# Hybrid decoder layer on one core: the sums of squares of the first half's tokens taken over features by TensorE in PSUM instead of by adds on VectorE and GpSimd

## The chip, the cores and the metric

The kernel runs on one core of one Trainium2 chip. Its engines are named as in the profile: PE (TensorE's matmuls) and PEld (its weight loads), DVE (VectorE), ACT (ScalarE), POOL (GpSimd) and SP (SyncE, which issues all of this kernel's DMAs). The metric is the time of one execution on the device in microseconds, the median of several runs, lower is better.

## The reference

One decoder layer over 2048 tokens of 1024 features, in float32. The step that matters here is the first line of the layer and what is multiplied by it:

```python
def rmsnorm(x, g):
    xf = x.astype(jnp.float32)
    y = xf * lax.rsqrt(jnp.mean(xf * xf, axis=-1, keepdims=True) + RMS_EPS)
    return (y * g.astype(jnp.float32)).astype(x.dtype)
...
h = rmsnorm(x, pre_g)
proj = h @ w_in
```

The columns of `proj` then feed three groups of heads: stick-breaking attention, sparse attention (an indexer scores all keys of a query, the best 256 are kept), and attention into 256 memory tokens. Their gated outputs go through one output projection, a second RMS norm and the residual. So for each token the sum of its 1024 squares must be formed, and its reciprocal root is a factor on everything the input projection yields.

## The kernel before

**Layout.** The input projection works on transposed tokens: `xT` has the features on the 128 partitions, in 8 tiles (`kt` = 0 to 7) of 128 features, and the tokens in 4 chunks `c` of 512. Each float32 operand is split into a high and a low part, and `three` multiplies hi by hi, hi by lo and lo by hi, so one output tile of 512 columns takes 8 x 3 = 24 matmuls into one PSUM bank. Banks are called `pp`, `pz`, `pT` and `po`, two of each; a unit whose tag has no free bank may borrow one of another tag.

**First half.** The program handles chunks 0 and 1 first (segment 0), then 2 and 3, then 0 and 1 again. `hprep_first` (L869) prepares a chunk of segment 0: for each `kt` it loads `xt`, makes `hi` (ACT or DVE) and `lo` (DVE) from x times the norm's weight, without the token's factor. Matmuls can thus start before any norm is known. Then it squares `xt` in place on ACT, adds the 8 squared tiles pairwise into two (`xs[0]`, `xs[1]`: even `kt` on DVE, odd on POOL), and lets PE sum these two over the partitions: for each of the 4 blocks `j` of 128 tokens, two matmuls with the block of squares as the weights and one column of ones as the moving operand. The four sums per partition go through `rstd` (DVE, then a power on POOL), `spread` transposes them on PE into a tile that ACT copies to SBUF (`rb`), and only then can an output tile of segment 0 leave its PSUM bank (`ev_split`, `nat_a`). Chunks 2 and 3 get their factors in another way (`factors`, L924: ACT squares `x` in token order, tiles named `Q`, and accumulates along the row).

**What runs around it.** `SEGMENTS` (L137) lists the units. In segment 0: `i0`, `i1` (the indexer's queries, four output tiles for the two chunks), then `q0` and `k0` together and `a0` (natural order, four token blocks, each 24 matmuls of 296 columns into one bank, then an eviction of eight steps by ACT and DVE), then `a1` and the rest.

**What sets the order.** The code yields operations; `Plan.run` (L518) is a list scheduler that prices each of them (L346; an fp32 matmul at 222 ns at the least) and emits, for each engine, one fixed order before anything runs. `either` offers an operation to two engines. Line L501 emits every operation, so nearly all rows of the profile name that line, and operations are told apart by their tiles. On the chip each engine goes through its list in order, and waits on semaphores.

**Names.** In the rows, `A`, `B` hold `xT` tiles and their squares, `H` the hi and lo parts, `R` the weights of `i0`, `i1`, `S` those of `q0`, `k0`, `V` and `W` those of `a0`, `Q` the raw loads (weights `wt`, or `x` for `factors`), `E` the tiles of evictions and of `rb`, `C` the small tiles of sums and factors. Tiles of the pool `xr` hold `xT`: 12 slots for the 16 tiles of chunks 0 and 1, so the last four loads of chunk 1 wait until tiles of chunk 0 are free.

Of the kernel before, what the change touches and what calls it, by code (L numbers as in the profile page):

```python
# [11 lines left out]
F32 = mybir.dt.float32  # L12
# [5 lines left out]
OP = mybir.AluOpType  # L18
# [4 lines left out]
P = 128  # L23
# [16 lines left out]
def rd(ap):  # L40
    return ap.bitcast(F32)
# [526 lines left out]
class Net:  # L568
# [48 lines left out]
    def consts(self):  # L617
        nc, a = self.nc, self.a
        pk = self.cload("pack", [P, 305], a["c_pack"])
        at = 0  # L620

        def part(w):
            nonlocal at
            at += w
            return pk[:, at - w:at]

        self.ident, self.causal, self.zt, self.stp = part(P), part(P), part(NB), part(NB)
        self.kvg, self.iota8, self.g = part(1), part(8), part(8)
        self.ones = self.cst.tile([P, P], F32, name="ones")
        nc.vector.memset(self.ones, 1.0)  # L630
        self.half = self.cst.tile([P, 16], F32, name="half")
        nc.vector.memset(self.half, 0.5)
        self.mhalf = self.cst.tile([P, 16], F32, name="mhalf")
        nc.vector.memset(self.mhalf, -0.5)
        self.fill = self.cst.tile([P, 1], F32, name="fill")
        nc.vector.memset(self.fill, FILL)
        self.mneg = self.cst.tile([P, 1], F32, name="mneg")
        nc.vector.memset(self.mneg, NEGM)
        self.zero = self.cst.tile([P, 1], F32, name="zero")
        nc.vector.memset(self.zero, 0.0)  # L640
        warm = self.cst.tile([P, 1], F32, name="warm")
        nc.scalar.activation(warm, self.zero, AF.Sigmoid)
        self.flags = self.cst.tile([P, NB], F32, name="flags")
        nc.vector.memset(self.flags, 0.0)
        self.far = self.cst.tile([P, NB, 6], F32, name="far")
        nc.gpsimd.memset(self.far, 0.0)
        c = lambda n, s, dt=F32: self.cst.tile(list(s), dt, name=n)
        self.identr = c("identr", [P, P], F32R)
        self.notyet = c("notyet", [P, P], F32R)
        self.iwt = [c(f"iw{k}", [P, 4, 8]) for k in range(NCH)]  # L650
# [218 lines left out]
    def hprep_first(self, c):  # L869

        pl = self.pl
        xs, H = [], []
        for kt in range(8):
            hi = yield Alloc("hh", [P, 512], F32R)
            lo = yield Alloc("hl", [P, 512], F32R)
            xt = yield Alloc("xr", [P, 512], F32)
            yield pl.sp.dma_start(xt, self.a["xT"][kt * P:(kt + 1) * P, c * 512:(c + 1) * 512])
            g = self.g[:, kt:kt + 1]
            yield pl.either(pl.act.activation(hi, xt, AF.Identity, scale=g, prio=2 * c),
                            pl.dve.tensor_scalar(hi, xt, g, None, op0=OP.mult, prio=2 * c))  # L880
            yield pl.dve.scalar_tensor_tensor(lo, xt, g, rd(hi), op0=OP.mult, op1=OP.subtract, prio=2 * c)
            xs.append(xt)
            H.append((hi, lo))
        pl.objs["H", 0, c] = H
        rb = yield Alloc("ev", [P, 512], F32)
        for kt in range(8):
            yield pl.act.activation(xs[kt], xs[kt], AF.Square, prio=2 * c + 1)
            if kt > 1:
                eng = pl.pool if kt % 2 else pl.dve
                yield eng.tensor_tensor(xs[kt % 2], xs[kt % 2], xs[kt], op=OP.add, prio=2 * c + 1)  # L890
                pl.F(xs[kt])
        if c == 1:
            self.stage("x")
        ps = yield Alloc("pT", [P, 512], F32)
        for j in range(4):
            for x in range(2):
                yield pl.pe.matmul(ps[:, j:j + 1], xs[x][:, j * P:(j + 1) * P], self.ones[:, 0:1], start=x == 0, stop=x == 1,
                                   prio=0)
        pl.F(*xs[:2])
        ss = yield Alloc("sm4", [P, 4], F32)  # L900
        yield pl.dve.tensor_copy(ss, ps[:, 0:4], prio=0)
        pl.F(ps)
        r = yield from self.rstd(ss, 4, 1.0 / D)
        pl.F(ss)
        yield from self.spread(r, rb)
        yield pl.sp.dma_start(self.RB[c], rb, wt=[("RB", c)])
        pl.objs["r", c] = (r, rb)
        if c == 1:
            self.stage("r")
# [1137 lines left out]
```

## Time and profile before

| | us |
|---|---|
| median of 3 runs | 1440.29 (1438.8 to 1441.74) |
| the profiled execution, its own time | 1438.55 |
| its span on the core | 1436.7 |
| PE busy | 1357.6 (94% of the span) |
| DVE busy | 1129.8 (79%) |
| ACT busy | 962.0 (67%) |
| POOL busy | 505.7 (35%) |

The profiled execution is 1.85 us longer than its span, and 1.74 us below the median of the runs. PE is the busiest engine, but its idle time is not spread evenly: of the first 80 us it is busy for 55.9 us, and from 200 to 300 us for 97.4 of 100. The change lies wholly in the first 60 us.

### The profile page before, as it was taken

How to read it: one execution, taken by the hardware profiler on the slowest of the kernel's cores; microseconds unless marked ns; L12 is line 12 of the kernel's file. 1: busy time of each engine (PE TensorE's matmuls, PEld its weight loads, DVE VectorE, ACT ScalarE, POOL GpSimd, SP SyncE). 2: the span in 40 equal slices, each digit the busy share in tenths (PEclk: the TensorE clock that was granted, in tenths of full speed). 3: DMA queues.
4: the chain of work that ended last, by engine and by line, in shares of the span. 5: the costliest groups of instructions: out<-in, count | busy, mean ns of one | idle time of the engine just before them, and what ended most of it. 6: DMA issues, size and time to landing. Idle time of an engine off the chain costs nothing.

```text
span 1436.7 us, 25178 instructions
## 1 busy us (share of the span) xinstructions
PE 1357.6 (94%) x7662; PEld 1151.3 (80%) x7662; DVE 1129.8 (79%) x3244; ACT 962.0 (67%) x2158; POOL 505.7 (35%) x693
## 2 busy tenths in 40 slices
PE   7688899999999899999999998889999999999996
PEld 5576678888888688978888886678888889898885
DVE  5437889889888899989887757889978898896332
ACT  6436677768778787888777749888766656765121
POOL 5516612223333337223445533444223221221452
PEclk9899999999999999999999999999999999999998
DMA  7638545766966347455768659886645483522563
GB/s 262 222 101 244 171 139 162 211 184 196 266 178 200 114 143 224 141 165 153 237 195 257 175 190 298 277 260 183 223 134 169 149 254 92 173 71 88 163 193 102
DMA packets 222781, 264.26 MB, mean 184 GB/s; under 512 B 17670, under 2 KB 141996, under 8 KB 222636
## 3 DMA queue, kind: packets, MB, share of 16 engines
q1 hardware_dynamic: 222636, 262.56, 60.1%
q8 instruction: 63, 1.03, 0.3%
q14 instruction: 82, 0.67, 0.1%
HBM read 183.58 MB, written 78.91 MB: 183 GB/s over the span
## 4 chain that ended last, share of the span: by engine, by line
PE 73%; ACT 7%; DVE 7%; DMA 4%; issue 2%; POOL 1%; SPq 0%; ACTq 0%; DVEq 0%; POOLq 0%
PE pp L501 43%; PE po L501 11%; PE pz L501 10%; PE pT L501 9%; DVE K L501 1%; DVE A L501 1%; ACT E L501 1%; ACT J L501 1%; DVE E L501 1%; DVE D L501 1%; POOL H L501 1%; ACT A L501 1%; DMA Q<-wt 1%; ACT V L501 1%; DVE C L501 1%
## 5 line engine op out<-in xcount | busy, mean ns | idle before, releaser
L501 PE MATMUL pp<-H,R 128*128 128x512 f32 x2328 | 636.5, 401 | 12.5 <-ACT H L501 8.1
L501 PEld LDWEIGHTS pp<-H,R 128*128 128x128 f32 x2328 | 425.4, 190 | 92.3 <-ACT H L501 9.2
L501 POOL TENSOR_TENSOR R<-Q,R 128x512 fp32r<-128x512 f32 x80 | 103.7, 1298 | 211.4 <-DVE R L501 68.6
L501 ACT ACTIVATE pz<-pz 128x512 f32<-128x512 f32 (+3 forms) x234 | 118.8, 514 | 29.1 <-PE pz L501 27.7
L501 POOL TENSOR_TENSOR V<-S,U 128x256 f32<-128x256 bf16 x48 | 32.6, 679 | 184.1 <-DVE C L501 166.6
L501 PE MATMUL pp<-W,H 128*128 128x296 f32 (+1 forms) x448 | 93.0, 293 | 0.0
L501 PE MATMUL po<-K,B 128*128 128x256 f32 (+3 forms) x352 | 85.6, 305 | 4.6 <-ACT K L501 1.7
L501 ACT CAST K<-pT 128x512 fp32r<-128x512 f32 (+3 forms) x135 | 61.3, 465 | 37.5 <-PE pT L501 28.9
L501 ACT ACTIVATE J<-A,D 128x384 uint8<-128x384 f32 (+9 forms) x60 | 75.3, 1255 | 15.8 <-DVE D L501 15.2
L501 ACT ACTIVATE E<-pp 128x512 f32<-128x512 f32 (+2 forms) x85 | 48.2, 567 | 48.9 <-PE pp L501 46.9
L501 PE MATMUL pp<-V,H 128*128 128x296 f32 (+1 forms) x320 | 71.1, 297 | 9.2 <-DVE E L501 9.2
L501 PE MATMUL pT<-pack,T 128*128 128x128 f32 x326 | 75.8, 275 | 0.4 <-DVE D L501 0.4
L501 PEld LDWEIGHTS po<-K,B 128*128 128x128 f32 x352 | 60.4, 192 | 15.4 <-ACT K L501 3.2
L501 DVE SCALAR_TENSOR_TENSOR A<-pz,iw,A 128x512 f32<-128x512 f32 (+3 forms) x105 | 70.1, 668 | 3.2 <-ACT pz L501 0.3
L501 PEld LDWEIGHTS pp<-W,H 128*128 128x128 f32 x448 | 71.3, 189 | 0.9
L501 POOL TENSOR_TENSOR T<-T 128x384 f32<-128x384 f32 (+2 forms) x42 | 34.5, 822 | 97.5 <-DVE T L501 77.5
L501 PEld LDWEIGHTS pp<-V,H 128*128 128x128 f32 x320 | 53.6, 189 | 13.2 <-DVE E L501 12.7
L501 PE MATMUL pz<-K,B 128*128 128x512 f32 (+3 forms) x158 | 60.0, 387 | 3.4 <-DMA B<-iq 1.3
L501 PE MATMUL pz<-H,R 128*128 128x512 f32 x192 | 61.5, 412 | 0.4 <-DVE C L501 0.4
L501 DVE TENSOR_SCALAR D<-D 128x1 uint8<-128x1 f32 (+1 forms) x308 | 42.3, 164 | 20.4 <-ACT J L501 17.1
L501 POOL TENSOR_TENSOR R<-E,R 128x512 fp32r<-128x512 f32 x25 | 33.5, 1342 | 68.9 <-ACT R L501 50.8
L501 ACT ACTIVATE pT<-pT 128x512 f32<-128x512 f32 (+3 forms) x99 | 51.6, 524 | 8.5 <-PE pT L501 7.7
(499 smaller groups left out, 3852.1 us busy)
## 6 DMA issues: line engine op xcount, KB each, us to landing
Q<-wt SPq DMA_DIRECT2D x84, 256.0 KB, 4.1
B<-qd SPq DMA_DIRECT2D x19, 512.0 KB, 5.8
S<-qsb SPq DMA_DIRECT2D x34, 256.0 KB, 4.3
B<-vd SPq DMA_DIRECT2D x33, 256.0 KB, 3.3
gt<-E SPq DMA_DIRECT2D x32, 256.0 KB, 3.1
S<-vsb SPq DMA_DIRECT2D x30, 256.0 KB, 4.3
S<-ksb SPq DMA_DIRECT2D x29, 256.0 KB, 4.7
B<-iq SPq DMA_DIRECT2D x56, 128.0 KB, 3.8
```

The costliest lines, as they stand in the source:

```text
L501: o.fn(*o.args, **o.kw)
```

## The change

For chunks 0 and 1 the twelve adds on DVE and POOL go. Instead PE sums all eight squared tiles of a chunk into the same four PSUM columns: a matmul of a tile of zeros opens the accumulation and another closes it, and between them stand 8 x 4 matmuls with a block of squares as weights and one column of ones as the moving operand. Each tile of squares is released when its four matmuls are done. The bank `pT` is taken before the squares instead of behind the adds. The whole diff:

```diff
@@ -638,6 +638,8 @@
         nc.vector.memset(self.mneg, NEGM)
         self.zero = self.cst.tile([P, 1], F32, name="zero")
         nc.vector.memset(self.zero, 0.0)
+        self.zero4 = self.cst.tile([P, 4], F32, name="zero4")
+        nc.vector.memset(self.zero4, 0.0)
         warm = self.cst.tile([P, 1], F32, name="warm")
@@ -883,20 +885,18 @@
             H.append((hi, lo))
         pl.objs["H", 0, c] = H
         rb = yield Alloc("ev", [P, 512], F32)
+        ps = yield Alloc("pT", [P, 512], F32)
         for kt in range(8):
             yield pl.act.activation(xs[kt], xs[kt], AF.Square, prio=2 * c + 1)
-            if kt > 1:
-                eng = pl.pool if kt % 2 else pl.dve
-                yield eng.tensor_tensor(xs[kt % 2], xs[kt % 2], xs[kt], op=OP.add, prio=2 * c + 1)
-                pl.F(xs[kt])
+            if kt == 0:
+                yield pl.pe.matmul(ps[:, 0:4], self.ones, self.zero4, start=True, stop=False, prio=0)
+            for j in range(4):
+                yield pl.pe.matmul(ps[:, j:j + 1], xs[kt][:, j * P:(j + 1) * P], self.ones[:, 0:1], start=False, stop=False,
+                                   skip_group_check=True, prio=0)
+            pl.F(xs[kt])
+        yield pl.pe.matmul(ps[:, 0:4], self.ones, self.zero4, start=False, stop=True, prio=0)
         if c == 1:
             self.stage("x")
-        ps = yield Alloc("pT", [P, 512], F32)
-        for j in range(4):
-            for x in range(2):
-                yield pl.pe.matmul(ps[:, j:j + 1], xs[x][:, j * P:(j + 1) * P], self.ones[:, 0:1], start=x == 0, stop=x == 1,
-                                   prio=0)
-        pl.F(*xs[:2])
         ss = yield Alloc("sm4", [P, 4], F32)
         yield pl.dve.tensor_copy(ss, ps[:, 0:4], prio=0)
```

The scheduler lays the whole program anew. On PE the first 197 instructions become 249; behind them PE's order is the same as before, and so are those of POOL and SP behind their first 38 and 61. Numbers behind a name only tell buffers apart; a row with x16 stands for sixteen instructions.

On PE, chunk 0: before, seven of the eight sums of chunk 0 (`pT0<-ones`) stand behind the matmuls of `i0` and `i1` on `kt` 0 to 3 of that chunk (`pp1` and `pp0`), and those of chunk 1 (`pz`) follow.

```order
L501 MATMUL pp0_110<-H3_125,R_120 128x512
L501 MATMUL pp0_110<-H2_124,R_120 128x512 x2
L501 MATMUL pp0_110<-H3_125,R_120 128x512
L501 MATMUL pT0_114<-ones_80,A1_123 128x1 x7
L501 MATMUL pz0_112<-H5_130,R_120 128x512
L501 MATMUL pz0_112<-H4_129,R_120 128x512 x2
```

On PE, chunk 0, now: the sums stand between the matmuls of `i0` (`pp1`), with only ten of its 24 ahead of the last of them.

```order
L501 MATMUL pp1_113<-H0_123,R_122 128x512
L501 MATMUL pT0_116<-ones_80,A1_125 128x1 x4
L501 MATMUL pp1_113<-H0_123,R_122 128x512
L501 MATMUL pT0_116<-ones_80,A1_125 128x1 x4
L501 MATMUL pp1_113<-H1_124,R_122 128x512
L501 MATMUL pp1_113<-H0_123,R_122 128x512 x2
L501 MATMUL pT0_116<-ones_80,A1_125 128x1 x8
L501 MATMUL pT0_116<-ones_80,A2_128 128x1 x16
L501 MATMUL pT0_116<-zero4_92,ones_80 128x4
L501 MATMUL pp1_113<-H1_124,R_122 128x512
```

The sums of chunk 0 moved from behind 38 matmuls of 512 columns to behind ten.

On PE, chunk 1: before, its sums (`B0`) stand behind all four tiles of `i0` and `i1`, and `q0` (weights `S`) follows.

```order
L501 MATMUL pz1_113<-H7_133,R_120 128x512
L501 MATMUL pz1_113<-H6_132,R_120 128x512
L501 MATMUL pT0_114<-ones_80,B0_131 128x1
L501 MATMUL pT1_115<-pack_78,C_128 128x128 x4
L501 MATMUL pT0_114<-ones_80,B0_131 128x1 x7
L501 MATMUL pp1_111<-H0_121,S_407 128x512
```

On PE, chunk 1, now: they stand in one piece ahead of the last matmul of `i1` on chunk 0 (`pp0`) and of all 24 of `i1` on chunk 1 (`pz1`).

```order
L501 MATMUL pp0_112<-H3_127,R_122 128x512
L501 MATMUL pT0_116<-ones_80,B0_132 128x1 x16
L501 MATMUL pT0_116<-ones_80,A1_125 128x1 x16
L501 MATMUL pT0_116<-zero4_92,ones_80 128x4
L501 MATMUL pp0_112<-H2_126,R_122 128x512
L501 MATMUL pz1_115<-H4_130,R_122 128x512
```

Twenty-five matmuls of 512 columns moved from ahead of these sums to behind them.

On DVE, the eviction of `a0`'s first block: before, the scaling of `pz1` and a cast of `S` stand ahead of its three steps (`iw0`, `B4`, and `E1` from `pp0`).

```order
L501 SCALAR_TENSOR_TENSOR E3_140<-pz0_112,E2_138 128x512
L501 SCALAR_TENSOR_TENSOR E1_137<-pz1_113,E2_138 128x512
L501 CAST S_407<-Q_119 128x512
L501 TENSOR_SCALAR iw0_100<-pp0_110,C_128 128x8
L501 SCALAR_TENSOR_TENSOR B4_485<-pp0_110,C_128,B4_485 128x2x32
L501 SCALAR_TENSOR_TENSOR E1_515<-pp0_110,C_128,E1_515 128x2x64
```

On DVE, the same place now.

```order
L501 SCALAR_TENSOR_TENSOR E3_141<-pz0_114,E2_139 128x512
L501 TENSOR_SCALAR iw0_102<-pp0_112,C_142 128x8
L501 SCALAR_TENSOR_TENSOR B4_512<-pp0_112,C_142,B4_512 128x2x32
L501 SCALAR_TENSOR_TENSOR E1_138<-pz1_115,E2_139 128x512
L501 CAST S_447<-Q_121 128x512 x2
L501 SCALAR_TENSOR_TENSOR E1_550<-pp0_112,C_142,E1_550 128x2x64
```

The scaling of `pz1` and two casts moved into the middle of the eviction, ahead of its last step.

## Rows read from the trace of the kernel before

**Rows 1.** Busy time by stretch: length, PE, PEld, DVE, ACT, POOL, granted clock, DMA share, GB/s.

```profile
40.00:60.00 20.00, 12.88 (x55) 10.89 (x55) 10.03 (x15) 10.14 (x24) 14.79 (x12) 0.74 0.84 274
200.00:300.00 100.00, 97.43 (x495) 80.58 (x495) 89.33 (x331) 76.53 (x178) 25.89 (x35) 1.00 0.62 177
```

**Rows 2.** Timeline of PE: start, length, operation, count, idle time before it and its releaser.

```profile
20.13 2.38 PE L501 MATMUL pp<-H,R 128*128 128x512 f32 x7 [1.92 <-POOL R L501]
...
27.12 1.62 PE L501 MATMUL pT<-ones,A 128*128 128x1 f32 x14
...
32.01 8.21 PE L501 MATMUL pz<-H,R 128*128 128x512 f32 x35
46.41 0.59 PE L501 MATMUL pT<-ones,B 128*128 128x1 f32 x2 [6.20 <-DVE B L501]
...
48.88 3.15 PE L501 MATMUL pT<-ones,B 128*128 128x1 f32 x14 [0.93 <-POOL B L501]
51.90 4.21 PE L501 MATMUL pp<-H,S 128*128 128x512 f32 x10
55.94 0.60 PE L501 MATMUL pT<-pack,C 128*128 128x128 f32 x4
```

**Rows 3.** The columns of Rows 1, stretches in which the granted clock fell or rose.

```profile
20.00:24.00 4.00, 3.87 (x11) 3.03 (x12) 3.26 (x3) 4.00 (x11) 3.92 (x4) 0.67 1.01 372
24.00:28.00 4.00, 4.00 (x23) 3.52 (x21) 0.00 (x0) 2.58 (x7) 2.75 (x4) 0.90 0.92 323
...
40.30:46.40 6.10, 0.00 (x0) 0.00 (x0) 5.22 (x6) 6.00 (x14) 6.02 (x6) 0.91 0.76 280
...
48.80:52.00 3.20, 3.12 (x15) 3.12 (x15) 0.43 (x1) 0.40 (x2) 1.30 (x2) 0.50 0.95 275
52.00:56.00 4.00, 4.00 (x12) 3.08 (x12) 0.98 (x5) 0.00 (x0) 3.20 (x3) 0.56 0.88 245
```

**Rows 4.** Groups of PE, 11.1 to 14.5 us, then 14.5 to 18: busy us, mean ns.

```profile
L501 PE MATMUL pp<-H,R 128*128 128x512 f32 x9 | 4.0, 626 | 0.0
L501 PE MATMUL pp<-H,R 128*128 128x512 f32 x13 | 3.6, 414 | 0.4 <-ACT R L501 0.4
```

**Rows 5.** Timeline of ACT: first and last square of chunk 0 (A<-A), copy of its rb.

```profile
11.24 0.61 ACT L501 ACTIVATE A<-A 128x512 f32<-128x512 f32 x1
...
17.33 1.15 ACT L501 ACTIVATE A<-A 128x512 f32<-128x512 f32 x2
...
32.29 0.59 ACT L501 COPY E<-pT 128x512 f32<-128x512 f32 x1 [5.71 <-PE pT L501]
```

**Rows 6.** Timeline of all engines, 29 to 58 us: factor, weight loads and their split, scaling.

```profile
29.22 1.47 POOL L501 TENSOR_TENSOR C<-C,mhalf 128x4 f32<-128x4 f32 x1 [2.46 <-DVE C L501]
...
46.53 1.55 SPq L501 DMA_DIRECT2D Q<-wt  x3
...
49.86 0.43 DVE L501 CAST S<-Q 128x512 fp32r<-128x512 f32 x1 [2.22 <-DMA Q<-wt]
50.37 1.27 POOL L501 TENSOR_TENSOR S<-Q,S 128x512 fp32r<-128x512 f32 x1 [1.54 <-DVE S L501]
...
57.25 0.69 DVE L501 SCALAR_TENSOR_TENSOR E<-pz,E 128x512 f32<-128x512 f32 x1 [4.19 <-ACT E L501]
57.97 0.62 ACT L501 CAST E<-E 128x512 fp32r<-128x512 f32 x1 [0.76 <-DVE E L501]
```

**Rows 7.** The chain of waits that ended last: start, length, what.

```profile
45.28 2.46 ACT Q L501 x8
...
64.71 3.57 PE pp L501 x24
...
82.92 12.01 PE pp L501 x44
```

**Rows 8.** Timeline, 60 to 63 us: a split on POOL, first step of the first block's eviction.

```profile
60.30 1.29 POOL L501 TENSOR_TENSOR E<-E,E 128x512 fp32r<-128x512 f32 x1 [0.33 <-ACT E L501]
...
62.18 0.32 ACT L501 ACTIVATE B<-pp,C 128x64 fp32r<-128x64 f32 x1 [1.96 <-PE pp L501]
```

## Prediction

> **What bounds the kernel now.** I read the busy times by stretch first: PE is the bound where the bulk of the work is (97.43 of 100 us from 200 to 300), but not in the early part, where it is busy for 12.88 of 20 us from 40 to 60 [rows 1]. The change lies there and its lists are the old ones behind it, so what counts is by how much PE reaches the common part earlier or later. The mark I use is the matmul at 82.92, the first behind `a0` in the chain of waits [rows 7]; behind it every engine works through the same list and waits for PE or for what PE releases.
>
> In PE's timeline the early part reads so [rows 2]: the 96 matmuls of `i0` and `i1` (wide ones, 512 columns) end at 40.2 (32.01 + 8.21). Then PE waits 6.20 us for DVE's adds and 0.93 for POOL's, ends the sums of chunk 1 by 51.9 and starts `q0`. `a0`'s first block ends at 62.1, since its eviction starts at 62.18 [rows 8]; its next block starts at 64.71 [rows 7].
>
> The granted clock reads 0.67 from 20 to 24, 0.90 from 24 to 28, 0.91 from 40.3 to 46.4, 0.50 from 48.8 to 52 and 0.56 from 52 to 56 [rows 3]. As its levels are 1.0 (2.4 GHz) and 0.5 (1.2 GHz), this places its falls at about 21.4 and 45.3 and its returns at 24.8 and 55.5. Each fall came after PE had stood. The returns came 4.7 and 3.6 us after wide matmuls ran again (20.13 and 51.90) [rows 2]. What matters most: from 48.88 to 51.90 PE ran 14 instructions of sums without a pause, 3.12 us busy of 3.20, and the clock still stayed at 0.50 until 55.5 [rows 2, 3]. The sums did not bring it back, the wide matmuls did. Also, wide matmuls take 626 ns on the mean from 11.1 to 14.5 and 414 from 14.5 to 18 [rows 4]: at the start PE runs at the low level too, though nothing was recorded as granted there yet.
>
> **Prices.** One sum (fp32, 128 columns of weights, one column of ones) is two instructions in the trace: 14 took 1.62 us at the full clock, so 0.23 per sum, and 3.02 (from 48.88 to the next start at 51.90) at the half, so 0.43 [rows 2]. A wide matmul takes 0.235 at the full clock (35 in 8.21) and some 0.41 at the half (10 from 51.90 to 55.94, the last half microsecond at full). Four transposes take 0.60 [rows 2].
>
> **What is removed and added.** Twelve adds leave DVE and POOL; on the path they cost the two waits for them (6.20 and 0.93). PE gets 26 matmuls more per chunk: 32 sums and two of zeros instead of 8. No trace shows the 4-column ones; I take them for a sum, since it is the same load of 128 weights. At the full clock the 52 cost 12.0 us, at the half 22.4. Squares, powers and transposes stay. The memset on DVE costs nothing: DVE waits for its first loads right behind it. The last four `xT` loads now wait, in SP's queue, for PE's sums of chunk 0's first four tiles instead of for adds; by the steps below these end at 13.6 to 20.4, and ACT rounds what the loads bring only behind the copy of `rb` near 33, so they have 12 us to land.
>
> **The sum, chunk 0.** PE's list is now: six wide matmuls, then sums and four wide ones in turn, then the sums of `kt` 2 to 7, then the rest. The first square ends at 11.85 and the last by 18.5 [rows 5]. As the sums don't bring the clock up and only ten wide ones are spread over this stretch, I take it at the half clock. From 11.85: four sums 13.6, one wide 14.0, four sums 15.7, three wide 16.9, 24 sums and the closing one 27.7. PE runs without a wait, as the squares are ready by then; behind the sums in its list stand the other 14 matmuls of `i0` on this chunk, whose tiles came long ago. Then 13 of them; with 4.1 us (between 3.6 and 4.7) until the clock is back, ten at 0.41 and three at 0.235: 32.5. Transposes for the factor: 33.1 (the power, 1.47 [rows 6], ended by about 30.5). ACT's copy of `rb` follows, against 32.29 before [rows 5], and ACT, in order, holds the hi parts of chunk 1's last four tiles behind it; they come just in time for PE. 13 wide 36.15, the opening matmul and 35 wide 44.6. Before, PE was through with all 96 at 40.2; here 25 are left.
>
> **Chunk 1.** 33 sums from 44.6. The clock fell 5.1 us after the last wide matmul at 40.2, and 3.2 us after the one before the fall at 21.4; I take 4.2: 18 at full, 15 at the half, 55.2. `q0` waits for a chain behind the last wide one of `pp0` (0.41): DVE scales 0.69, ACT rounds 0.62 [rows 6], two squares of `factors` at 0.62 (four of them in 2.46 [rows 7]) free a slot, the load lands 3.3 us later (46.53 to 49.86), then 0.43 on DVE and 1.27 on POOL [rows 6], with hand-overs 8.3 in all: 63.5. PE itself needs ten wide at the half, 15 at full and eight transposes: 64.0. So `q0` starts at 64.0, against 51.9. PE has become what is late.
>
> **`a0`.** Now only 9 of `q0`'s 24 matmuls stand ahead of the first block, and 15 in its gaps, where before 20 and 4: 9 x 0.235, then 3.57 [rows 7], so the first block ends at 69.7: 7.6 later. Its eviction took 2.57 (62.14 to 64.71). In DVE's list the scaling of `pz1` and two casts now stand inside it, and its last steps write the slot that POOL still reads when it splits that scaled tile: 0.69 + 0.62 + 1.29 [rows 6, 8] come into it. Counted from the block's end: DVE's scaling 1.5 to 2.2, ACT's cast 2.9, POOL's split 4.2, the two last steps 5.0. That is 2.4 more; the later gaps stay at 2.57. PE stands behind that wait. Sum: 7.6 + 2.4 = 10.0 us.
>
> On the profiled execution, 1438.55, that makes 1448.5; the median of the runs lies 1.74 higher, which gives 1450.3. I predict 1449, between them. Bounds of the unknown costs: the returns of the clock at 3.6 or 4.7, the fall at 3.2 or 5.1, the added wait between 0.7 (if only the casts count) and 4: 1445 to 1454. I keep the middle, as the nearest rows are those of the same two instructions in the same stage.
>
> **Rivals.**
> 1. *The sums count as work for the clock* and it is full from 14.5 on, as before [rows 4]. Then chunk 0's sums end at 21.6, PE reaches chunk 1's at 36.8 and ends them at 44.4; the first weights of `q0` are split by 52.7, the first block ends at 57.9, 4.2 earlier, and with the added wait the gain is 1.8; from the median (as for all three) 1438.5, not slower. It decides if PE is through with chunk 1's sums before about 46. For it: PE has no idle time of seven microseconds left at 40. Against it: the 14 sums that ran at 0.50 without lifting it [rows 3]. The Trainium skill, "TensorE: Matmul & The Clock Gate", section "What's actually happening", says that the clock follows how busy PE has been recently; read by issue time that would give this rival's 1438.5, but the 3.12 busy us of 3.20 at 0.50 speak against reading it so.
> 2. *They hold a full clock but don't raise it.* Chunk 0 as in the forecast, chunk 1's sums all at 0.23: through at 52.1, first block's end at 65.6, 3.5 later; plus 2.4: 1446.2. No row shows sums for long enough after wide ones to exclude it.
> 3. *The delay is given back later.* Behind the mark PE still waits now and then for DVE and POOL; if these run ahead during PE's extra time, 7 us or more of the 10 would have to vanish: 1442. Against it: those waits are for work on what PE has just produced.
>
> **How the numbers follow.** Forecast 0.56, rival 1 0.17, rival 2 0.17, rival 3 0.10. A measurement of this kernel tells some 0.2% (2.9 us) from no change. Slower by more: the forecast, nearly all of rival 2 and a little of 3, 0.73; faster by more: the better third of rival 1, 0.06, and 0.01 for more; the same: the rest, 0.20. Range: down to rival 1's edge at 1437.5, up to the forecast's upper bound, 1454.
>
> **What would show it.** In the changed kernel: sums of chunk 0 at about 0.43 each, ending near 28; the copy of `rb` near 33; chunk 1's sums starting near 44 at full clock and ending near 55 at half; the first matmul of `q0` near 64; five microseconds between `a0`'s first and second block; the matmul that stood at 82.92 near 93. If the granted clock reads 1.00 during the sums, rival 1 or 2 holds. If the mark comes near 93 and the end still moves by less than 3 us, rival 3 does.

## The result

The changed kernel takes 1453.74 us (median of four runs, 1452.72 to 1456.59) against 1439.69 of the kernel before (1438.8 to 1441.74): a ratio of 1.0098, 95% interval 1.0080 to 1.0116, 14 us more. The prediction, 1449 in a range of 1437.5 to 1454, named the sign, the place and the mechanism; its point lies 4.7 us too low, and the result lies 0.3 us inside the upper end of the range. The profiled execution took 1452.72 us with a span of 1450.9, against 1438.55 and 1436.7.

The busy times of the page, after (engine, busy us, share of the span, instructions):

```profile
PE 1378.6 (95%) x7766; PEld 1173.0 (81%) x7766; DVE 1119.7 (77%) x3240; ACT 961.7 (66%) x2157; POOL 491.9 (34%) x687
```

DVE has 10 us less to do than before and POOL 14, PE 21 more. That is what the change says, and none of the saved time shows in the result: PE's two waits for the adds, 7.1 us together [rows 2], are gone, but the work that PE took over costs it more than that.

PE's timeline after, the early part (start, length, operation, count, idle time before and its releaser; a one-column sum is two instructions). It answers to [rows 2]:

```profile
16.49 10.23 PE L501 MATMUL pT<-ones,A 128*128 128x1 f32 x48
26.58 0.57 PE L501 MATMUL pT<-zero,ones 128*128 128x4 f32 x2
27.01 5.06 PE L501 MATMUL pp<-H,R 128*128 128x512 f32 x13
...
43.54 3.63 PE L501 MATMUL pT<-ones,B 128*128 128x1 f32 x32
47.03 6.06 PE L501 MATMUL pT<-ones,A 128*128 128x1 f32 x32
52.95 0.57 PE L501 MATMUL pT<-zero,ones 128*128 128x4 f32 x2
53.38 0.77 PE L501 MATMUL pp<-H,R 128*128 128x512 f32 x1
...
62.36 2.25 PE L501 MATMUL pp<-H,S 128*128 128x512 f32 x9
...
66.50 1.39 PE L501 MATMUL pp<-W,H 128*128 128x296 f32 x9
67.73 0.86 PE L501 MATMUL pp<-H,S 128*128 128x512 f32 x3
70.97 0.73 PE L501 MATMUL pp<-H,S 128*128 128x512 f32 x2 [2.39 <-DVE S L501]
73.52 0.61 PE L501 MATMUL pp<-V,H 128*128 128x296 f32 x1 [1.81 <-DVE E L501]
```

From 8.3 to 68 us PE now never waits: it is the bound of a stretch in which it had stood for 6.2 us at one place alone. Chunk 0's sums have moved further than was said of the change: in PE's timeline of before seven of the eight stand behind 48 wide matmuls, not 38, and here the last of them stands behind ten. Chunk 0's last 24 sums take 0.42 us each (10.09 / 24). Of chunk 1's, the first 16 take 0.22 each (3.49 / 16), the other 16 take 0.37 on the mean (5.92 / 16).

The granted clock, after (stretch, its length, busy time of PE, PEld, DVE, ACT, POOL, granted clock, DMA share, GB/s):

```profile
46.00:48.00 2.00, 2.00 (x20) 2.00 (x19) 0.06 (x1) 1.18 (x5) 1.02 (x1) 1.00 0.94 280
48.00:50.00 2.00, 2.00 (x12) 2.00 (x11) 0.00 (x0) 0.42 (x2) 0.00 (x0) 0.51 0.87 287
...
56.00:58.00 2.00, 2.00 (x6) 1.53 (x5) 0.30 (x1) 1.46 (x6) 0.97 (x1) 0.50 0.36 99
58.00:60.00 2.00, 2.00 (x11) 1.64 (x11) 0.17 (x1) 0.20 (x1) 0.00 (x0) 0.93 0.91 327
...
72.00:74.00 2.00, 0.48 (x2) 0.48 (x3) 0.35 (x1) 0.88 (x2) 2.00 (x3) 0.50 0.26 100
...
90.00:92.00 2.00, 2.00 (x9) 2.00 (x9) 0.00 (x0) 0.00 (x0) 0.00 (x0) 0.50 0.19 55
```

It falls at 48.0, in the middle of chunk 1's sums, while PE is busy for every bit of the time, and is back at 58.3, 4.9 us after wide matmuls run again at 53.38. It falls once more near 72, after PE has stood from 68.6 but for two matmuls, and again near 89, in `a0`'s fourth block. (Up to 48 the column reads 1.00 throughout; that the sums of chunk 0 ran at the low level is read from their 0.42 us.)

The chain of waits after (start, length, what), and the last group of the one before:

```profile
63.39 6.47 DMA rb<-E
73.52 5.89 PE pp L501 x24
81.92 3.55 PE pp L501 x24
87.97 5.08 PE pp L501 x24
95.56 12.07 PE pp L501 x44
...
1334.89 103.37 PE pp L501 x456
```

```profile
1321.81 103.39 PE pp L501 x456
```

Set beside [rows 7], this gives the sum. `a0`'s first block ends at 67.9 (66.50 + 1.39) against 62.1: +5.8. From there to its second block it takes 5.6 us against 2.6: +3.0. The second block itself takes 5.89 against 3.57: +2.3. The fourth takes 5.08 against 3.56: +1.5. Together 12.6, and the mark has moved from 82.92 to 95.56, 12.6. At the last group of matmuls the shift is 13.1. The last 1.1 us lie behind it: from the start of that group to the end of the span it is 114.9 us before and 116.0 after; in the kernels below whose list is the same there it lies between 114.9 and 116.6, so this bit tells nothing of the change.

### The profile page after: what moved, and what is told of

Same layout as the page of the kernel before. It is cut to its first block, busy times and chain, and to the rows that moved or that the text cites. A ratio compares the mean times of both kernels' runs of the same rounds, so it can differ in the third digit from the quotient of the medians.

```text
span 1450.9 us, 25363 instructions
## 1 busy us (share of the span) xinstructions
PE 1378.6 (95%) x7766; PEld 1173.0 (81%) x7766; DVE 1119.7 (77%) x3240; ACT 961.7 (66%) x2157; POOL 491.9 (34%) x687
## 4 chain that ended last, share of the span: by engine, by line
PE 76%; ACT 8%; DVE 6%; DMA 5%; issue 2%; POOL 1%; SPq 1%; ACTq 0%; DVEq 0%; POOLq 0%
PE pp L501 44%; PE po L501 11%; PE pz L501 11%; PE pT L501 10%; ACT E L501 1%; DVE E L501 1%; DVE K L501 1%; ACT A L501 1%; ACT J L501 1%; DVE D L501 1%; SPq L501 1%; DVE A L501 1%; POOL H L501 1%; DMA B<-iq 1%; ACT V L501 1%
## 5 line engine op out<-in xcount | busy, mean ns | idle before, releaser
L501 ACT ACTIVATE J<-A,D 128x384 uint8<-128x384 f32 (+9 forms) x60 | 79.1, 1319 | 18.2 <-DVE D L501 17.7
L501 DVE SCALAR_TENSOR_TENSOR A<-pz,iw,A 128x512 f32<-128x512 f32 (+3 forms) x91 | 62.6, 688 | 2.6 <-ACT pz L501 0.2
L501 PEld LDWEIGHTS pp<-V,H 128*128 128x128 f32 x320 | 55.5, 195 | 11.0 <-DVE E L501 10.5
```

What stands on the lines that cost most here:

```text
L501: o.fn(*o.args, **o.kw)
```

## The experiments

Each kernel was timed against the kernel before on the same chip. The mark is the group of 44 matmuls behind `a0`, 82.92 before and 95.56 after; it shows the early part alone. It is read from one execution of each kernel and wanders by itself: in kernels whose PE list is that of before up to there, the 96 wide matmuls end at 40.2 (before), 39.3 (before_own), 39.5 (c1_only), 39.6 (mix3) and 37.6 (mix3_own). So single microseconds of the mark tell nothing.

| kernel | what differs | ratio to before, 95% | mark |
|---|---|---|---|
| after | | 1.0098 (1.0080 to 1.0116) | 95.56 |
| c0_only | sums on PE for chunk 0 alone | 1.0063 (1.0040 to 1.0086) | 90.79 |
| c1_only | sums on PE for chunk 1 alone | 1.0064 (1.0040 to 1.0088) | 92.09 |
| skip24 | after's lists, a quarter of the sums | 1.0012 (0.9996 to 1.0028) | 83.95 |
| wide | after's lists, sums of 512 columns | 1.0011 (0.9998 to 1.0024) | 85.05 |
| w32 | the same, exact, lists laid anew | 1.0021 (1.0004 to 1.0038) | 85.33 |
| price | after, sums priced at 430 ns | 1.0024 (1.0013 to 1.0036) | 87.34 |
| late3 | after, sums at a lower priority | 1.0037 (1.0020 to 1.0055) | 91.31 |
| own | after, a slot more for `pz1` | 1.0055 (1.0035 to 1.0075) | no such group |
| mix3 | chunk 0 adds, chunk 1 512 columns | 1.0021 (1.0002 to 1.0039) | 85.34 |
| mix3_own | mix3 and own | 1.0168 (1.0148 to 1.0187) | 77.07 |
| before_own | before, a slot more for `pz1` | 0.9963 (0.9952 to 0.9974) | 79.59 |

### Is it the sums, or the order that they bring?

In skip24 the planner lays out the changed kernel, and 24 of each chunk's 32 sums are left out when the lists are emitted:

```diff
-                yield pl.pe.matmul(ps[:, j:j + 1], ..., prio=0)
+                o = pl.pe.matmul(ps[:, j:j + 1], ..., prio=0)
+                if kt < 6:
+                    o.alts = [o.alts[0][:1] + ((lambda *args, **kw: None),) + o.alts[0][2:]]
+                yield o
...
-        r = yield from self.rstd(ss, 4, 1.0 / D)
+        r = yield from self.rstd(ss, 4, 4.0 / D)
```

> Every engine's list is that of the changed kernel, but 24 of each chunk's 32 sums (tiles 0 to 5) are not emitted; the factor is formed from two of the eight tiles, so the norm is an estimate and the output differs. Theory (what PE spends on the sums, most of it at the half clock, makes the delay): PE reaches chunk 1's sums near 38 and is through with them near 41, a0's first block ends 10 to 12 us earlier than the changed kernel's 67.7, and the time is 1439 to 1443. Rival (the order of the lists costs the time, not the sums): the first block ends at most 4 us earlier, time 1449 or more.

Nearly the whole loss is gone: ratio 1.0012, mark 83.95. PE's timeline of skip24:

```profile
16.79 3.57 PE L501 MATMUL pT<-ones,A 128*128 128x1 f32 x16 [4.20 <-ACT A L501]
...
37.57 1.95 PE L501 MATMUL pT<-ones,A 128*128 128x1 f32 x16
...
56.36 1.39 PE L501 MATMUL pp<-W,H 128*128 128x296 f32 x9
...
62.70 0.59 PE L501 MATMUL pp<-V,H 128*128 128x296 f32 x1 [1.77 <-DVE E L501]
```

So PE's time on the sums makes the loss. But look at the rest: `a0`'s first block ends at 57.75, 4.4 us earlier than in the kernel before, and the mark is still 1 us later. Some five microseconds are lost in `a0`: its first two blocks stand 4.95 us apart instead of 2.57, and the second and the fourth take 5.1 us each instead of 3.6. The changed kernel's order of `a0` is a cost of its own, taken up further down.

### Is it the low clock?

Wide keeps all lists as well. Each tile's four one-column sums become one fp32 matmul of 512 columns, ones as the weights and the squares streaming; the matmuls of zeros go:

```diff
+                if j < 3:
+                    o.alts = [o.alts[0][:1] + ((lambda *args, **kw: None),) + o.alts[0][2:]]
+                else:
+                    o.alts = [o.alts[0][:3] + ((ps, self.ones, xs[kt]), {"start": kt == 0, "stop": kt == 7}) + o.alts[0][5:]]
```

> Every engine's list is that of the changed kernel, but each tile's four sums (one column each) are replaced by one fp32 matmul of 512 columns, with ones as the weights and the squares as the moving operand, and the two matmuls of zeros are left out. The factor is then read from the first four columns, so each token is scaled by another token's norm and the output differs. Theory (sums of one column leave PE at its low clock, wide ones raise and hold it): from the four transposes of 128 columns in 0.60 us I estimate 0.6 to 0.9 us for one at the full clock, 5 to 7.5 per chunk; chunk 0's end near 20 instead of 27, chunk 1's start near 37 and end by 44, granted clock 1.00 there, q0 starts 10 us or more earlier than 62.4, the time is 9 to 13 us below the changed kernel's. Rival (the clock falls whatever stands there, or these matmuls cost as much as the sums): less than 5 us below.

PE's timeline of wide, then its granted clock:

```profile
16.69 5.52 PE L501 MATMUL pT<-A,ones 128*128 128x512 f32 x12
...
36.42 3.60 PE L501 MATMUL pT<-B,ones 128*128 128x512 f32 x8
39.85 3.60 PE L501 MATMUL pT<-A,ones 128*128 128x512 f32 x8
42.88 0.79 PE L501 MATMUL pp<-H,R 128*128 128x512 f32 x1
...
50.24 0.73 PE L501 MATMUL pp<-H,S 128*128 128x512 f32 x2 [0.19 <-DVE S L501]
```

```profile
36.00:40.00 4.00, 4.00 (x12) 2.00 (x11) 0.00 (x0) 4.00 (x9) 1.22 (x2) 1.00 0.53 193
40.00:44.00 4.00, 4.00 (x13) 1.96 (x12) 0.70 (x4) 2.23 (x8) 1.02 (x1) 1.00 0.72 234
44.00:48.00 4.00, 4.00 (x21) 3.35 (x20) 0.95 (x3) 3.14 (x9) 1.71 (x2) 1.00 0.55 175
```

Chunk 1's sums take 6.5 us (36.42 to 42.88) and the clock stays at 1.00. The one-column sums would have taken 7.2 at the full clock (33 x 0.218), so the work is nearly the same in time; they took 9.8 (43.54 to 53.38). Chunk 0's end at 21.6 instead of 27.0. The wide matmuls behind run at the full clock too, `q0` starts at 50.24 instead of 62.36, and 10.5 of the 12.6 us at the mark are gone. The theory held in its numbers, and the rival (less than 5 us) fell: it is the low clock, of the sums and of what follows them. Though it sums all the squares, wide ends `a0`'s first block at 56.77, no later than skip24 with a quarter of the sums, and 11 us earlier than the changed kernel; that this is 5.4 us earlier than before and the mark still 2 us later is again the order of `a0`.

The Trainium skill, "TensorE: Matmul & The Clock Gate", section "What's actually happening", says that the clock follows how busy PE has been recently. This trace does not agree if busy is read off the profile: PE was busy without a pause in both kernels, and the clock fell under the one form and stayed up under the other.

A first try at the same question went wrong. Fed put one matmul of 504 columns behind each four sums of chunk 1:

```diff
+            fn(ps[:, 8:512], hi[:, 0:P], hi[:, 0:504], start=True, stop=True, skip_group_check=True)
```

> The changed kernel with eight matmuls more: in chunk 1 one matmul of 504 columns, whose result nobody reads, stands behind each four sums; all lists are otherwise the same. Theory (the clock falls because sums of one column do not hold it, wide matmuls do): all 33 sums of chunk 1 take 0.22, the granted clock stays 1.00 from 43 to 60, the sums end near 52.6 though there is more work, the 25 wide matmuls behind run at full, and q0 starts near 59.5 instead of 62.4; the time is 2 to 4 us below the changed kernel's. Rival (the fall at 48 has another cause, or one wide matmul in nine does not hold the clock): the sums end at 53.4 + 1.9 to 3.3, and the time is 2 to 3 us above it.

These matmuls started an accumulation of their own in the bank in which the sums were open, which spoilt the sums (nobody reads their result, so nothing else in the edit can change the output); the run took 3795.77 us, I take it by the kernel's general path, and its time tells nothing. The early part of its trace does, for it lies ahead of the damage:

```profile
44.00:48.00 4.00, 4.00 (x30) 3.80 (x29) 0.34 (x2) 3.16 (x10) 1.02 (x1) 0.88 0.49 154
48.00:52.00 4.00, 4.00 (x19) 3.91 (x18) 0.00 (x0) 0.19 (x2) 0.00 (x0) 0.50 0.52 178
```

The clock fell all the same, near 47 (0.88 over the first stretch). One wide matmul behind eight instructions of sums did not hold it. My expectation missed here, its rival was right.

### One chunk alone

In c0_only the changed loop runs for chunk 0 and the loop before for chunk 1; in c1_only the condition is `c == 1`.

```diff
+        if c == 0:
+            ps = yield Alloc("pT", [P, 512], F32)
...
+        else:
+            for kt in range(8):
+                yield pl.act.activation(xs[kt], xs[kt], AF.Square, prio=2 * c + 1)
+                if kt > 1:
...
```

> Only chunk 0 is summed by PE, chunk 1 by adds as before. Theory (the delay comes where PE, behind both chunks' sums, reaches the common part later than DVE's adds had let it before): PE loses some 9 us on chunk 0, but before it stood from 40.2 to 48.9 anyway, so it reaches chunk 1's last sums near 50 to 55 instead of 51.9; the first eviction of a0 still takes the scaling of pz1 in; the matmul that stood at 82.92 comes at 82 to 86, the time is 1438 to 1443. Rival (each chunk's sums cost their own PE time): half of the 14 us, about 1447. Chunk 0's sums at 0.42 us each in both.

> Only chunk 1 is summed by PE; the order on PE up to the last matmul of i1 is that of before, and the 34 instructions of sums stand behind it in one piece, ahead of a0. Theory: they start near 40.2 at 0.22 each, the clock falls some 4.5 us later, the rest takes 0.42, they end near 50, and a0's first block follows from about 52 at the half clock; time 1436 to 1441. Rival (each chunk's sums cost their own PE time): about 1447. If the clock stayed full through the sums they would end at 47.6.

Both missed. Each alone costs 9 us, where the two together cost 14, so the loss is not a sum over chunks: the rival's 1447 is nearer to the numbers than the theory's range, but its reason, half of the 14 for each, does not hold. Chunk 0's sums took 0.42 each in c0_only (24 in 10.1), chunk 1's in c1_only started at 40.55, were half way at 44.47 and over at 51.73, where I had expected 50: the sums went nearly as expected. What I had missed is in PE's timeline behind `a0`'s first block, c0_only and then c1_only:

```profile
52.02 1.62 PE L501 MATMUL pT<-ones,B 128*128 128x1 f32 x14
...
64.18 1.22 PE L501 MATMUL pp<-H,S 128*128 128x512 f32 x2 [7.99 <-DVE S L501]
67.06 4.27 PE L501 MATMUL pp<-H,S 128*128 128x512 f32 x10 [1.67 <-POOL S L501]
```

```profile
61.76 1.22 PE L501 MATMUL pp<-H,S 128*128 128x512 f32 x2 [3.07 <-DVE S L501]
```

In both, the first block stands ahead of `q0`, and DVE's casts of `q0`'s weights stand inside the block's eviction; `q0`'s matmuls, 12 or 24 of them ahead of the second block, wait for them. In c0_only DVE in turn waited 8.63 us for ACT's last squares of `factors`. I had seen these places in the lists and priced them at nothing.

### The order of `a0`

Own gives the scaled tile of `i1` on chunk 1 a slot of another pool, so that it need not wait for the slot which the store of `rb` and `a0`'s eviction use:

```diff
-            t = yield Alloc("ev", [P, 512], F32)
+            t = yield Alloc("xh" if name == "IQ" and u == 1 and c == 1 else "ev", [P, 512], F32)
```

> The changed kernel, but the scaled tile of i1 on chunk 1 gets a slot of its own (tag xh), so that it does not wait for the slot that the store of rb and then a0's eviction use. The sums are the same, in the same place on PE; DVE's list has the scaling of pz1 ahead of the first eviction, and 12, 25 and 8 matmuls of q0 and k0 stand in the gaps between a0's blocks. Theory (about half of the loss stands in a0's evictions and the clock that falls in their gaps): chunk 1's sums still end near 53.4, a0's first gap is filled, and the time is 5 to 10 us below the changed kernel's. Rival (what is lost is lost in the sums): within 3 us of the changed kernel's. The rest of the program is laid anew here, so single microseconds of the time are not told apart, the early part by the trace is.

> The kernel before with the same slot of its own for the scaled tile of i1 on chunk 1, and nothing else. a0's first block then stands ahead of q0, whose matmuls fill the first two gaps with 16 and 8. Theory (the gaps of a0 are worth filling, whatever the sums do): the first gap of 2.57 us is hidden and most of the second, less some half clock in the first block: the matmul that stood at 82.92 comes near 79 to 80, the time is 2 to 4 us below the kernel before. Rival (q0's weights are late and its matmuls wait in the gaps): no gain, up to 3 us slower.

In own the sums are as in the changed kernel (chunk 1's end at 53.17), and `a0`'s gaps are filled: at 92.02 its PE has 24 matmuls of `k0` behind it that the changed kernel has not begun at 95.56, worth 5.6 us, so the early part is some 9 us ahead. Of these 6 are left in the time (1.0055 against 1.0098); the rest of the program is another here, and gave 3 back.

Before_own is the clean one, since PE's list behind the mark is that of the kernel before. Its timeline of PE:

```profile
56.44 3.90 PE L501 MATMUL pp<-H,S 128*128 128x512 f32 x16
...
63.48 2.02 PE L501 MATMUL pp<-H,S 128*128 128x512 f32 x8
...
66.16 0.40 PE L501 MATMUL pp<-V,H 128*128 128x296 f32 x1 [0.66 <-DVE E L501]
```

The first gap is covered by 16 matmuls, the second by 8 but for 0.66 us, and the mark stands at 79.59, 3.3 earlier. (PE is through with the 96 wide matmuls 0.9 us earlier here, ahead of anything that the slot touches, so some 2.4 us of the 3.3 are `a0`'s.) The time is 0.9963 of the kernel before: 1436.85 against 1441.13 on that chip, 4 to 5 us. So this one line, which has nothing to do with the sums, beats both kernels.

### Can the place on PE be mended?

Late3 gives the sums the priority of the matmuls around them (`prio=3` for `prio=0`), price corrects the planner's number:

```diff
-                return max(222.0, 4 * n / 2.2 + 3), 0.0
+                return (430.0 if n <= 4 else max(222.0, 4 * n / 2.2 + 3)), 0.0
```

> The changed kernel with the one-column sums at the priority of the matmuls around them instead of above. Chunk 0's sums then stand among the wide matmuls, chunk 1's behind all 96 of i0 and i1; q0's stand in a0's gaps (11, 9, 4). Theory (what counts is the clock at which the sums run, so their neighbours): chunk 0's sums run at 0.22 as far as wide matmuls stand close ahead of them; chunk 1's start near 42, the clock falls some 4.5 us later and they end near 52 instead of 53.4, with nothing left to do behind them; but the weights of q0 wait for casts in the first eviction again, so 1445 to 1450. Rival (the sums' early place alone makes the loss): at or below the kernel before.

> The changed kernel with one number of the planner changed: it reckons 430 ns for an fp32 matmul of at most four columns, what they took at the half clock, instead of 222. The sums then stand in two blocks, chunk 0's behind six wide matmuls, chunk 1's behind 26, both at the half clock but for their first microseconds; a0's gaps hold 7, 7, 7 and 3 matmuls of q0. Theory: PE's time on the sums stays as in the changed kernel, so it gets through i0 and i1 no earlier than 58 to 62, but the gaps of a0 cost 4 to 6 us less: 1446 to 1450. Rival (the wrong price was the whole trouble): within 3 us of the kernel before.

PE's timeline of price:

```profile
11.35 13.81 PE L501 MATMUL pT<-ones,A 128*128 128x1 f32 x64
...
57.72 5.60 PE L501 MATMUL pz<-H,R 128*128 128x512 f32 x24
...
66.44 1.79 PE L501 MATMUL pp<-H,S 128*128 128x512 f32 x7
69.13 0.40 PE L501 MATMUL pp<-V,H 128*128 128x296 f32 x1 [0.90 <-DVE E L501]
```

The sums cost what they cost (0.43 each for chunk 0), and PE is through with `i0` and `i1` at 63.3, a microsecond later than in the changed kernel. Yet the ratio is 1.0024. With other prices the scheduler put 7, 7, 7 and 3 matmuls of `q0` into `a0`'s gaps, so that PE stands 0.90 us in each, and the clock reads 1.00 from 52 on. The mark is 8.2 us earlier than in the changed kernel, with the same sums at the same cost. I had expected 4 to 6 us from the gaps and forgotten, as in the prediction, what the clock in the blocks is worth; the result lies near the rival's, for a reason that is not the rival's. Late3's time came out as expected (1.0037, about 5 us), but chunk 1's sums stand from 46.98 to 56.7, five microseconds later than I thought: chunk 0's sums let the clock fall, and 12 wide matmuls behind them took 5.09 us. `q0` then waits 4.77 us for its weights.

### Wide sums, done properly

W32 sums with eight fp32 matmuls of 512 columns, copies the row of sums to SBUF and turns it into columns by four small matmuls; mix3 does that for chunk 1 alone, where PE had stood, and mix3_own adds the slot.

```diff
+            yield pl.pe.matmul(ps, self.ones, xs[kt], start=kt == 0, stop=kt == 7, prio=0)
+            pl.F(xs[kt])
...
+        yield pl.dve.tensor_copy(rb[0:1, :], ps[0:1, :], prio=0)
+        for j in range(4):
+            yield pl.pe.matmul(ps[:, j:j + 1], rb[0:1, j * P:(j + 1) * P], self.ones[0:1, 0:1], start=True, stop=True, prio=0)
```

> The sums as fp32 matmuls of 512 columns with ones as weights (8 per chunk), priced as such by the planner, exact: the row of sums is copied to SBUF by DVE and turned into columns by four small matmuls. Theory: the clock stays up as in the kernel with wide sums on the changed lists; PE's work on sums is 5 to 7.5 us per chunk, no adds on DVE and POOL; 14 matmuls of q0 stand ahead of a0 and 10 in the first gap. The time lies 10 to 15 us below the changed kernel's, that is from 3 below to 4 above the kernel before. Rival (with sums on PE the lists cost what the adds had saved): 5 us or more above the kernel before.

> Chunk 0 by adds as before; chunk 1 by eight fp32 matmuls of 512 columns on PE (exact; row copied by DVE, turned by four small matmuls), at the priority of the work around. In the kernel before, PE stood 6.2 us there for DVE's adds. Theory: the sums follow ACT's squares (41 to 45.2 before) at 0.86 each and end near 48.5 instead of 51.9, with the granted clock at 1.00 to the end of a0's first block instead of 0.50 from 48.8; but the scaling of pz1 and the casts of q0's weights stand inside the first eviction again, so q0's 18 matmuls behind block 1 wait for weights. The matmul that stood at 82.92 comes at 78 to 82, the time is 1 to 5 us below the kernel before. Rival (the order of the first eviction eats the gain, as with one-column sums on chunk 1 alone): 0 to 5 us above it.

> As the kernel with wide sums on chunk 1 alone, with the slot of its own for the scaled tile of i1. The early part should gain another 2 to 4 us (scaling ahead of the eviction, 2, 10, 7 and 4 matmuls of q0 in the gaps); the rest of the program is laid anew, which cost the changed kernel with its own slot some 5 us. Theory: early part 4 to 8 us ahead of the kernel before, time from 6 below to 2 above it. Rival (no gain in the early part): at least 3 above.

W32 did what was expected: 1.0021, 11 us better than the changed kernel and no better than adds. Mix3 has PE's timeline

```profile
41.42 2.84 PE L501 MATMUL pT<-B,ones 128*128 128x512 f32 x6 [1.78 <-ACT B L501]
...
45.39 3.60 PE L501 MATMUL pT<-A,ones 128*128 128x512 f32 x8
...
56.56 0.73 PE L501 MATMUL pp<-H,S 128*128 128x512 f32 x2 [2.69 <-DVE S L501]
59.25 6.65 PE L501 MATMUL pp<-H,S 128*128 128x512 f32 x16 [1.96 <-POOL S L501]
```

PE is through with the eight matmuls at 49.0 instead of 51.9, about as expected. The factor gains less, for the copy of the row and the four small matmuls follow: DVE reads the columns at 51.09, against 52.07 before. All of the gain is lost on the casts of `q0`'s weights in the first eviction: the rival. Mix3_own reaches the mark at 77.07, 5.9 us ahead of the kernel before, of which 2.7 stand already at the end of the 96 wide matmuls, ahead of the changed place. Its median lies 22.5 us above that of the kernel before (ratio 1.0168), so all of the loss stands behind the mark, where the scheduler lays the program another way; what costs the time there was not followed up. The faster early part was worth nothing.

## Why the prediction was right, and where it was off

| step | predicted | trace |
|---|---|---|
| chunk 0's sums end | 27.7 | 27.0 |
| chunk 1's sums start, end | 44.6, 55.2 | 43.5, 53.4 |
| clock falls in them after | 4.2 | 4.5 |
| clock back after they end | 4.1 | 4.9 |
| `q0` starts | 64.0 | 62.4 |
| `a0`'s first block ends | 69.7 (+7.6) | 67.9 (+5.8) |
| from there to the second block | 5.0 (+2.4) | 5.6 (+3.0) |
| second and fourth block | 3.57 (+0) | 5.89 and 5.08 (+3.8) |
| the mark | near 93 (+10) | 95.56 (+12.6) |

**The price of a sum** at either level of the clock was read from eight of them in the trace of before, and held for 64 within some 5% (0.42 and 0.22, against 0.43 and 0.23). **That the sums would not bring the clock up** was read from one row in which PE was busy for 3.12 of 3.20 us at 0.50 [rows 3]; wide shows that this was the point of the whole case. Rivals 1 and 2, in which the sums raise the clock or hold it, fall with the 0.51 at 48 to 50, and rival 1 also with the 0.42 us of chunk 0's sums. Rival 3, that the delay is given back, falls with 12.6 at the mark and 13.1 at the last matmuls.

**Sized too large:** the way to the first block, by 1.8 us. Chunk 0's sums ended 0.7 us earlier than forecast, mostly because they began at 11.37 instead of 11.85: the first square now ended at 10.64. The stretch between the chunks was 0.4 us shorter, and chunk 1's sums took 9.8 us instead of 10.6: about 0.3 of that is the clock, which held for 4.5 us instead of 4.2, the rest the price of a sum.

**Sized a little too small:** the first eviction, 5.6 us for 5.0, since it began behind a wait that I had not counted. I counted the scaling of `pz1`, ACT's cast and POOL's split, and took the scaling to start 1.5 us after the block. All engines, after:

```profile
62.97 0.85 SPq L501 DMA_DIRECT2D rb<-E  x2
...
69.88 0.69 DVE L501 SCALAR_TENSOR_TENSOR E<-pz,E 128x512 f32<-128x512 f32 x1 [0.52 <-DMA rb<-E]
...
71.36 1.32 POOL L501 TENSOR_TENSOR E<-E,E 128x512 fp32r<-128x512 f32 x1 [5.12 <-ACT E L501]
...
73.11 0.35 DVE L501 SCALAR_TENSOR_TENSOR E<-pp,C,E 128x128 fp32r<-128x128 f32 x1 [1.55 <-ACT E L501]
```

The scaling started 2.0 us after the block's end, since its slot was still being read by the store of `rb`, 6.47 us under way in a DMA queue that was full: the share of the DMA engines reads 1.02 and 1.04 from 66 to 70. That store ended last, not DVE's order: without the 0.52 us of waiting for it the scaling would have started at the 1.5 of the forecast.

**The step that failed:** "the later gaps stay at 2.57". The gaps did; the blocks between them did not. I had moved the whole pattern of `a0` along in time and left its clock as it was. Behind the longer gap the clock reads 0.50 from 72 on, so the second block ran at the low level, 2.3 us longer. The fourth caught a fall as well, 1.5 us, and there no longer gap explains it: PE waits 2.52 us ahead of it in both kernels, and in the kernel before the clock stayed up:

```profile
70.00:83.00 13.00, 7.66 (x53) 7.14 (x53) 2.07 (x7) 3.62 (x13) 0.00 (x0) 0.99 0.14 42
```

A block behind a wait of 2.52 us also takes 5.08 us in c1_only (its third and fourth), skip24, wide and mix3, so in this place the clock may fall or not; what decides it stays open. Together that is 3.8 us, more than the whole point error at the mark, 2.6. For the first of the two I had the row that said so: the clock at 45.3 fell after PE had stood, too.

So the errors have opposite signs, -1.8 against +0.6 and +3.8, and it is luck that the point was nearer than its largest term. Of the 4.7 us by which it was too low, 2.6 stand at the mark, 0.4 come up to the last group of matmuls, 1.1 behind it, and the rest from setting the point between the time of one execution and the median. That the placement was a separate cost, which skip24 and price show, was in the prediction as the 2.4 us of one eviction; in skip24 and price the early part shows it to be worth 5 to 8 us, the clock included.

## What to carry to other kernels

What a sum over partitions cost PE here hung on the form of its matmuls: the same squares took about the same time at the full clock in one-column and in 512-column matmuls, but only the second kept the clock, for themselves and for what came behind. Work that a change moves onto the bounding engine is priced at the clock which that engine will then have, and a wait that grows is priced with the half-clock stretch behind it. And where a scheduler lays out a program, see what it did elsewhere: one slot more was worth more here than the sums, and a better start was lost entirely when the rest was laid anew.

## What the runs showed of the hardware that I had not expected

- An fp32 matmul of 512 columns took 0.86 us at the full clock (four from 36.42 to 39.85 in wide), four sums of one column 0.87 (16 from 43.54 to 47.03 after).
- PE can be busy without a pause for 9.8 us and lose its clock in the middle: 1.00 up to 48.0, 0.50 up to 58.
- A matmul that starts an accumulation in other columns of a bank spoilt the open sums in columns 0 to 3 of it. The Trainium skill, "PSUM — Partial Sum Buffer", section "The four PSUM rules", says that such a start clears the whole bank's marks of what was written; the run agrees in its outcome.
